# Expert weights in halves of a matrix, four neighbouring rows per partition, into pairs of slots

## The chip, the core and the metric

The kernel runs on one core of a Trainium2 chip. The core has a matrix engine (TensorE, PE in the profile), a vector engine (DVE), an activation engine (ACT, ScalarE), POOL, and a sync engine (SP) that here does nothing but issue DMAs. Sixteen DMA engines move data between HBM and the on-chip memory of 128 partitions. The metric is the time of one execution in microseconds (us).

## What is computed

Two layers, each a mixer over 256 latent and 256 context tokens of width 1024, and then 16 experts. Each expert picks 32 tokens of a stream and has three matrices of 1024 x 1024 in f32, 4 MB each. The part that the change touches:

```python
def expert_choice_ffn(h, w_router, w_g, w_u, w_d):
    ...
    aff = jax.nn.softmax(logits, axis=1)
    gate, idx = lax.top_k(aff, cap)
    xs = h[bi, idx]
    a = jnp.einsum('becd,edf->becf', xs, w_g)
    u = jnp.einsum('becd,edf->becf', xs, w_u)
    y = jnp.einsum('becf,efd->becd', jax.nn.silu(a) * u, w_d)
    return jnp.zeros_like(h).at[bi, idx].add(y * gate[..., None].astype(y.dtype))
```

In layer 0 the experts work on the latent and the context stream, in layer 1 (the last) on the latent stream alone. Before the experts comes, in each layer, `x = x + gt1 * latent_mixer(...)`: an input projection (`w_in`), attention and a short convolution, a projection per branch (`w_branch`) and an output projection (`w_out`). The modulation vectors of both come from `w_ada`.

## The kernel before

All weights pass through one arena (class `Arena`): 21 slots of 1 MB (8 KB in each partition), in the last layer's experts 22. The free slots stand in one queue and are used in the order in which they came free. `load` puts a weight's key into a list; `pump` issues the next loads of the list on SP's queue as long as a slot is free and fewer than `cap` loads are held. `cap` is set by `limit` from the table `LIMIT` (line 36) at a few points of a layer: 13, 14 and 10 around and in the experts of layer 0, 16, 17 and 17 in layer 1. A slot comes free when the last instruction that reads it has run (`done`, `give`); the DMA that takes it waits for that instruction. The list has a fixed order: the mixer's weights (`load_mixer`), then the experts' (`load_experts`), layer by layer. In the trace an expert's loads stand at L65 (one run of 8 KB per partition), all others at L68.

An expert matrix is loaded in four quarters of 256 rows (`rows`): partition p gets rows 2p and 2p + 1 of a quarter, so one packet carries 8 KB. The last expert's quarters come as two DMAs of 512 KB (4 KB rows), and the last layer's last down matrix in column halves (2 KB rows). Order of the list within expert e: gate and up quarters 1 to 3 of e, gate and up quarter 0 of e + 1, the four down quarters of e.

TensorE computes gate and up products (`gate_up`, tile gu, L1183: 8 matmuls in layer 0 for each of 8 steps k), transposes them (guT, L1280), and multiplies with the down matrix (`down` and the loop after it, tile py, L1313 in layer 0, L1232 in layer 1); xg (L1128) gathers the tokens for four experts, sc (L1216) adds the results back. Its order is written out by hand for the experts (`manual_schedule`). Since partition p holds neighbouring rows, step k has to read features in the same order: `feats(k)` picks every second column of 256. In the mixers each weight is first split into a high and a low part, `wh` on ACT (L469) and `wl` on DVE (L470), ahead of the matmuls (L439 to L441).

## Time and profile before

| | |
|---|---|
| median of 3 runs | 1789.51 us (1789.15 to 1790.28) |
| profiled execution | 1790.62 us, its span 1788.9 us |
| TensorE busy | 1628.1 us, 91% of the span |
| VectorE, ScalarE busy | 736.4 and 499.5 us |
| read from HBM | 531.21 MB, 298 GB/s over the span |
| expert loads of 1 MB | 360, 19.8 us from issue to landing (median) |

The span runs from the first to the last instruction of the profiled execution; the durations further down are from that execution, and its own time is 1.7 us longer than the span. Shares of busy time are averages over both layers' mixers and experts, so the stages are read one by one: the page cuts the span into 40 slices of 44.7 us, and a window gives the busy time, the DMA share and the rate of a stretch.

### The profile page before, as it was taken

The numbers are of one execution on the slowest core, as the hardware profiler recorded it, in microseconds if no ns is written. First come the engines' busy times: TensorE is split into PE (matmuls) and PEld (weight loads), VectorE is DVE, ScalarE is ACT, GpSimd is POOL, SyncE is SP. The second block draws the span as 40 slices with busy tenths as digits, with TensorE's granted clock in tenths as the row PEclk, the third lists the DMA queues.
The fourth block names the chain that finished last, engine by engine and source line by source line (L and its number), as shares of the span: only waits on it lengthen the run. The fifth ranks groups of instructions, "written<-read, shape, count | busy, mean of one in ns | idle before, by whom it ended". The sixth has DMA issues, their size and how long they took to land.

```text
span 1788.9 us, 23088 instructions
## 1 busy us (share of the span) xinstructions
PE 1628.1 (91%) x9134; PEld 905.5 (51%) x9134; DVE 736.4 (41%) x1678; ACT 499.5 (28%) x1081; POOL 0.6 (0%) x6
## 2 busy tenths in 40 slices
PE   7999999999999999989998899999989777778777
PEld 4886676777774343423423268878953212112111
DVE  4786775235444122221121359876662111112122
ACT  4564454223332111100101247655531000000000
POOL 0000000000000000000000000000000000000000
PEclk9999999999999999999999999999999999999999
DMA  9301124753969999999999981328788999999998
GB/s 347 111 26 48 48 71 165 236 153 118 368 226 375 391 420 421 421 421 421 421 421 419 400 321 67 118 71 238 269 337 361 421 421 421 421 421 421 422 419 338
DMA packets 131775, 533.77 MB, mean 298 GB/s; under 512 B 12452, under 2 KB 21076, under 8 KB 85588
## 3 DMA queue, kind: packets, MB, share of 16 engines
q1 hardware_dynamic: 129024, 529.90, 75.9%
q10 hardware_dynamic: 2644, 2.40, 0.4%
q8 instruction: 72, 1.18, 0.3%
q14 instruction: 35, 0.29, 0.0%
HBM read 531.21 MB, written 1.05 MB: 298 GB/s over the span
## 4 chain that ended last, share of the span: by engine, by line
PE 56%; DMA 38%; DVE 3%; ACT 2%; issue 1%; ACTq 0%; SPq 0%; DVEq 0%
DMA s<-in_w_e_up_dram 29%; DMA s<-in_w_e_down_dram 8%; PE pf L439 7%; PE pf L440 7%; PE pf L441 7%; PE gu L1183 6%; PE O L837 3%; PE S L775 2%; PE ada L306 2%; PE PTp L811 2%; PE pt L439 2%; PE pt L441 2%; PE pt L440 2%; PE sc L1216 2%; PE py L1313 2%; PE xg L1128 2%
## 5 line engine op out<-in xcount | busy, mean ns | idle before, releaser
L1183 PE MATMUL gu<-s,s 128*64 128x512 f32 (+1 forms) x1536 | 330.2, 613 | 54.7 <-DMA s<-in_w_e_up_dram 45.2
L440 PE MATMUL pf<-s,wh 128*128 128x512 f32 (+1 forms) x768 | 263.9, 344 | 0.0
L439 PE MATMUL pf<-s,wh 128*128 128x512 f32 (+1 forms) x768 | 262.9, 343 | 0.0
L441 PE MATMUL pf<-s,wl 128*128 128x512 f32 (+1 forms) x768 | 262.2, 343 | 0.0
L470 DVE TENSOR_TENSOR wl<-s,wh 128x512 fp32r<-128x512 f32 x272 | 186.0, 688 | 160.6 <-ACT wh L469 142.8
L469 ACT ACTIVATE wh<-s 128x512 fp32r<-128x512 f32 x272 | 170.4, 630 | 277.2 <-PE pf L440 193.5
L1183 PEld LDWEIGHTS gu<-s,s 128*64 128x64 f32 (+1 forms) x1536 | 90.3, 129 | 264.8 <-issue 144.5
L439 PEld LDWEIGHTS pf<-s,wh 128*128 128x128 f32 x768 | 146.1, 190 | 22.7 <-issue 5.2
L441 PEld LDWEIGHTS pf<-s,wl 128*128 128x128 f32 x768 | 145.9, 190 | 14.9 <-issue 1.8
L440 PEld LDWEIGHTS pf<-s,wh 128*128 128x128 f32 x768 | 146.3, 191 | 13.8 <-issue 0.7
L1250 ACT ACTIVATE gu<-gu 128x512 f32<-128x512 f32 x48 | 28.6, 596 | 400.6 <-PE gu L1183 400.6
L1232 PE MATMUL py<-s,aT 128*32 128x512 f32 x512 | 88.7, 624 | 39.3 <-DMA s<-in_w_e_down_dram 38.0
L1313 PE MATMUL py<-s,aT 128*32 128x512 f32 x1024 | 114.2, 594 | 2.4 <-DMA s<-in_w_e_down_dram 1.7
L1216 PE MATMUL sc<-ys,SP 128*128 128x512 f32 x192 | 93.3, 618 | 10.6 <-ACT SP L1158 7.9
L1218 DVE TENSOR_TENSOR s<-s,sc 128x512 f32<-128x512 f32 x96 | 65.9, 687 | 73.8 <-PE sc L1216 73.7
L1208 DVE TENSOR_TENSOR ys<-py,s 32x512 f32<-32x512 f32 x64 | 44.0, 687 | 126.6 <-PE py L1313 125.7
L1183 PE MATMUL gu<-s,XS 128*32 128x512 f32 x512 | 78.4, 637 | 18.1 <-DMA s<-in_w_e_up_dram 13.6
L1284 DVE TENSOR_TENSOR aT<-aT,guT 128x256 f32<-128x256 f32 x48 | 20.1, 421 | 161.7 <-ACT aT L1283 160.9
L1158 ACT ACTIVATE SP<-OGT 128x256 f32<-128x256 f32 x16 | 6.1, 383 | 265.3 <-PE OGT L1156 265.3
L1313 PEld LDWEIGHTS py<-s,aT 128*32 128x32 f32 x1024 | 31.1, 109 | 83.4 <-issue 71.1
L1204 DVE TENSOR_TENSOR ys<-py,s 128x512 f32<-128x512 f32 x32 | 20.7, 686 | 124.4 <-PE py L1232 124.4
L1232 PEld LDWEIGHTS py<-s,aT 128*32 128x32 f32 x512 | 17.5, 110 | 106.9 <-DMA s<-in_w_e_down_dram 70.5
(208 smaller groups left out, 1911.1 us busy)
## 6 DMA issues: line engine op xcount, KB each, us to landing
s<-in_w_e_gate_dram SPq DMA_DIRECT2D x120, 1024.0 KB, 19.8
s<-in_w_e_up_dram SPq DMA_DIRECT2D x120, 1024.0 KB, 19.8
s<-in_w_e_down_dram SPq DMA_DIRECT2D x120, 1024.0 KB, 19.8
s<-in_w_ada_dram SPq DMA_DIRECT2D x48, 1024.0 KB, 11.7
s<-in_w_in_dram SPq DMA_DIRECT2D x46, 1024.0 KB, 7.0
s<-in_w_branch_dram SPq DMA_DIRECT2D x16, 512.0 KB, 10.2
s<-in_w_out_dram SPq DMA_DIRECT2D x8, 1024.0 KB, 7.4
s<-in_w_e_gate_dram SPq DMA_DIRECT2D x16, 512.0 KB
```

The source lines that it names most:

```text
L439: PE.matmul(ps, lh, rh, start=start, stop=False)
L440: PE.matmul(ps, lh, rl, start=False, stop=False)
L441: PE.matmul(ps, ll, rh, start=False, stop=stop)
L469: ACT.activation(hi, w[:, kk, :], AF.Copy)
L470: DVE.tensor_tensor(out=lo, in0=w[:, kk, :], in1=hi.bitcast(F32), op=OP.subtract)
L837: PE.matmul(O[64 * kv:64 * kv + 64], v[:, k0 + kt, c0:c0 + 64], ipt[kv][1][:, kt].rearrange("p g q -> p (g q)"), start=(kt == 0), stop=(kt ...
L1183: PE.matmul(gps[fh % nf][r0:r0 + NC], XG[e // 4][1][:, k, e % 4, :], w[a][:, k % 2, 512 * fh:512 * fh + 512], start=(k == 0), stop=(k == 7))
L1208: DVE.tensor_tensor(out=ys[s][r, hs_], in0=py[r, e % 2, :], in1=g2[s][r, hs_], op=OP.mult)
L1216: PE.matmul(po, w, ys[s][:, hs_], start=True, stop=True)
L1218: DVE.tensor_tensor(out=o, in0=o, in1=po, op=OP.add)
L1232: PE.matmul(py[r0:r0 + 32, h, :], aT[:, ff, :], rhs, start=(ff < 4), stop=(ff >= 4))
L1313: PE.matmul(py[r0:r0 + 32, e % 2, :], aT[:, ff, 32 * s:32 * s + 32], w[:, ff % 2, 512 * h:512 * h + 512], start=(ff == 0), stop=(ff == 7))
```

## The change

A matrix is loaded in two halves of 512 rows; partition p gets rows 4p to 4p + 3 of a half, so a packet carries 16 KB and a load 2 MB. The 21 slots become ten pairs, p0 to p9, and one single slot; a load of an expert half takes a whole free pair (`take_two`), 1 MB loads take the free half of a pair that is already open if there is one (`take`). `cap` counts slots; in layer 1 it is 18 in place of 17. `feats`, the router's weights, the ffn's bias and gain vectors (`wst`, `wt`) follow the new order of features; two more small transposes at the start prepare them. In layer 1 the hand-written order of the steps is kept by calling `gate_up` for two steps at a time. The last expert's halves come in four DMAs of 512 KB, 4 KB rows as before, and all gate parts of a half come ahead of its up parts. The last down matrix keeps its 2 KB rows. Cut to its core:

```diff
-LIMIT = [(8, 2, 13, 14, 10), (8, 6, 16, 17, 17)]
+LIMIT = [(8, 2, 13, 14, 10), (8, 6, 16, 18, 18)]
...
+    def open(self, j, dtype):
+        self.tiles[j] = (self.pool.tile([128, 4096], dtype, name=f"p{j}", tag=f"pair{j}"), dtype)
+
+    def fits(self, i, dtype):
+        j = i // 2
+        return i >= self.n // 2 * 2 or j not in self.tiles or self.tiles[j][1] == dtype
+
+    def take(self, shape, dtype, name, alone=False):
+
+
+        ok = [i for i in self.free if self.fits(i, dtype)]
+        pairs = [i for i in ok if i < self.n // 2 * 2]
+        single = [i for i in ok if i not in pairs]
+        i = next((k for k in pairs if k // 2 in self.tiles), (pairs or single)[0])
+        if alone and single:
+            i = single[0]
+        self.free.remove(i)
+        return i, self.view(i, shape, dtype)
...
+    def drop(self, us):
+        self.free.extend(us)
+        for i in us:
+            if i ^ 1 in self.free and i // 2 in self.tiles:
+                del self.tiles[i // 2]
+
+    def take_two(self):
+
+        seen = set()
+        for i in self.free:
+            if i ^ 1 in seen and i < self.n // 2 * 2:
+                a = i & ~1
+                self.free.remove(a)
+                self.free.remove(a + 1)
+                return a
+            seen.add(i)
+        return None
...
+    def load_rows(self, key, w, parts):
+
+        self.queue.append((key, w.rearrange("(p k) f -> p k f", k=4), parts, 2))
...
+            w, parts = shape, src
+            a = self.take_two()
+            if a is not None:
+                us = [a, a + 1]
+            else:
+                us = ([i for i in self.free if self.fits(i, F32)] if force else self.odd())[:2]
+                if len(us) < 2:
+                    return False
...
+                whole = self.tiles[a // 2][0]
+            ts = [self.view(u, [128, 2, D], F32) for u in us]
+            if parts > 1:
+                for k in range(4):
+                    self.nc.sync.dma_start(out=ts[k // 2][:, k % 2], in_=w[:, k])
+            elif a is not None:
+                self.nc.sync.dma_start(out=whole, in_=w.rearrange("p k f -> p (k f)"))
+            else:
...
-        while self.queue and self.free and len(self.ready) < self.cap:
-            self._issue()
+        while self.queue and len(self.free) >= self.queue[0][3] and self.held + self.queue[0][3] <= self.cap:
+            if not self._issue():
+                return
...
-    def rows(key, w, q, parts):
-
-        w = w[256 * q:256 * q + 256]
-        if parts == 1:
-            ar.load(key, [128, 2, D], w.rearrange("(p k) f -> p (k f)", k=2), "p k f -> p (k f)")
-        else:
-            w = w.rearrange("(p k) f -> p k f", k=2)
-            ar.load(key, [128, 2, D], [((slice(0, 128), i), w[:, i]) for i in range(2)])
 
...
-                rows((nm, l, e, q), w[l, e], q, 2 if e == NE - 1 else 1)
+                ar.load_rows((nm, l, e, q), w[l, e, 512 * q:512 * q + 512], 2 if e == NE - 1 else 1)
 
         up(0, 0)
         for e in range(NE):
 
             parts = 2 if e == NE - 1 else 1
-            for q in range(1, 4):
-                up(e, q)
+            up(e, 1)
             if e + 1 < NE:
                 up(e + 1, 0)
-            if (l, e) != (DEPTH - 1, NE - 1):
-                for q in range(4):
-                    rows(("d", l, e, q), w_e_down[l, e], q, parts)
-                continue
-            for h in range(2):
-                w = w_e_down[l, e, :, 512 * h:512 * h + 512].rearrange("(q p k) f -> q p k f", p=128, k=2)
-                for i in range(2):
-                    ar.load(("d", l, e, h, i), [128, 4, 512],
-                            [((slice(0, 128), slice(2 * q, 2 * q + 2)), w[2 * i + q]) for q in range(2)])
+            for i in range(2):
+                w = w_e_down[l, e, 512 * i:512 * i + 512]
+                if (l, e) != (DEPTH - 1, NE - 1):
+                    ar.load_rows(("d", l, e, i), w, parts)
+            if (l, e) == (DEPTH - 1, NE - 1):
+                for h in range(2):
+                    w = w_e_down[l, e, :, 512 * h:512 * h + 512].rearrange("(q p k) f -> q p k f", p=128, k=4)
+                    for i in range(2):
+                        ar.load(("d", l, e, h, i), [128, 4, 512], w[i])
...
-        return slice(256 * (k // 2) + k % 2, 256 * (k // 2) + 256, 2)
+        return slice(512 * (k // 4) + k % 4, 512 * (k // 4) + 512, 4)
...
-        for i in range(4):
-            q.dma_start(out=wr[:, 2 * i:2 * i + 2, 0:NE],
-                        in_=w_router[l, 256 * i:256 * i + 256].rearrange("(p k) e -> p k e", k=2))
+        for i in range(2):
+            q.dma_start(out=wr[:, 4 * i:4 * i + 4, 0:NE],
+                        in_=w_router[l, 512 * i:512 * i + 512].rearrange("(p k) e -> p k e", k=4))
...
-        def gate_up(e, q, ks=(0, 1)):
+        def gate_up(e, q, ks=(0, 1, 2, 3)):
             if q == 0 and 0 in ks:
                 for f0 in range(nf):
                     gps[f0] = pmm([128, 512], "gu")
             keys = [(nm, l, e, q) for nm in ("g", "u")]
             w = [ar.get(key) for key in keys]
-            for k in (2 * q + i for i in ks):
+            for i in ks:
+                k = 4 * q + i
                 for fh in range(2):
                     for a in range(2):
                         r0 = NC * (a + 2 * (fh // nf))
                         PE.matmul(gps[fh % nf][r0:r0 + NC], XG[e // 4][1][:, k, e % 4, :],
-                                  w[a][:, k % 2, 512 * fh:512 * fh + 512], start=(k == 0), stop=(k == 7))
-            if 1 in ks:
+                                  w[a][i][:, 512 * fh:512 * fh + 512], start=(k == 0), stop=(k == 7))
+            if 3 in ks:
                 for key in keys:
                     ar.done(key)
 
         one_hot(0)
         gather(0, 0)
         gate_up(0, 0)
-        gate_up(0, 1)
...
-            for q in range(2 if e == 0 else 1, 4):
-                gate_up(e, q)
-
-                if last and e and q == (1 if e == NE - 1 else 2):
+            if e:
+                gate_up(e, 0, (2, 3))
+
+                if last:
+                    if e < NE - 1:
+                        gate_up(e, 1, (0, 1))
                     way_back(e - 1)
                     scatter(e - 1, 0)
                     scatter(e - 1, 1)
+            gate_up(e, 1, (2, 3) if last and 0 < e < NE - 1 else (0, 1, 2, 3))
...
-                for q in (0, 2):
+                for q in range(2):
                     for h in range(2):
-                        down(e, py, h, (q, q + 1))
-                    for i in (q, q + 1):
-                        ar.done(("d", l, e, i))
+                        down(e, py, h, (q,))
+                    ar.done(("d", l, e, q))
             else:
-                for q in range(4):
+                for q in range(2):
                     w = ar.get(("d", l, e, q))
-                    for ff in range(2 * q, 2 * q + 2):
+                    for ff in range(4 * q, 4 * q + 4):
                         for h in range(2):
                             for s in range(ns):
                                 r0 = 32 * block(e, s, h)
                                 PE.matmul(py[r0:r0 + 32, e % 2, :], aT[:, ff, 32 * s:32 * s + 32],
-                                          w[:, ff % 2, 512 * h:512 * h + 512], start=(ff == 0), stop=(ff == 7))
+                                          w[ff % 4][:, 512 * h:512 * h + 512], start=(ff == 0), stop=(ff == 7))
                     ar.done(("d", l, e, q))
             for h in range(2):
```

On TensorE, ACT and DVE the order of the instructions stays as it was but for the two transposes and a few neighbours that change places. What moves is SP's row of loads. Names are tiles: s8 is slot 8, p1 pair 1, the number behind it a running number, which says how late in the program the load stands.

SP, the first expert loads of layer 0, before: each goes into a slot that a mixer weight left.

```order
L68 DMA s4_4287<-in_w_ada_dram 128x4x512
L65 DMA s8_4289<-in_w_e_gate_dram 128x2048
L65 DMA s9_4308<-in_w_e_up_dram 128x2048
L65 DMA s10_4374<-in_w_e_gate_dram 128x2048
L65 DMA s3_4503<-in_w_e_up_dram 128x2048
L65 DMA s19_4505<-in_w_e_gate_dram 128x2048
L65 DMA s20_4549<-in_w_e_up_dram 128x2048
L65 DMA s6_4551<-in_w_e_gate_dram 128x2048
L65 DMA s1_4568<-in_w_e_up_dram 128x2048
```

SP, the same place after: each takes a pair, eight different ones, and then p1 and p0 a second time.

```order
L129 DMA p7_2701<-in_w_ada_dram 128x4x512
L151 DMA p1_4282<-in_w_e_gate_dram 128x4096
L151 DMA p0_4415<-in_w_e_up_dram 128x4096
L151 DMA p6_4459<-in_w_e_gate_dram 128x4096
L151 DMA p3_4476<-in_w_e_up_dram 128x4096
L151 DMA p5_4489<-in_w_e_gate_dram 128x4096
L151 DMA p8_4511<-in_w_e_up_dram 128x4096
L151 DMA p9_4596<-in_w_e_down_dram 128x4096
L151 DMA p7_4598<-in_w_e_down_dram 128x4096
L151 DMA p1_4638<-in_w_e_gate_dram 128x4096
L151 DMA p0_4659<-in_w_e_up_dram 128x4096
```

The first load has moved to about where the second stood, but is twice as large, and the second half matrix (p0_4415) stands behind the third quarter.

SP, the end of layer 1's mixer, before: all mixer loads (the last are `w_ada`) stand ahead of the experts'.

```order
L68 DMA s14_9727<-in_w_out_dram 128x4x512
L68 DMA s10_9867<-in_w_ada_dram 128x4x512
L68 DMA s19_9945<-in_w_ada_dram 128x4x512
L68 DMA s3_9947<-in_w_ada_dram 128x4x512
L65 DMA s6_9949<-in_w_e_gate_dram 128x2048
L65 DMA s2_9951<-in_w_e_up_dram 128x2048
L65 DMA s12_9953<-in_w_e_gate_dram 128x2048
```

SP, the same place after:

```order
L151 DMA p5_9612<-in_w_e_up_dram 128x4096
L129 DMA p9_6807<-in_w_out_dram 128x4x512
L129 DMA p3_9160<-in_w_out_dram 128x4x512
L129 DMA p2_4539<-in_w_ada_dram 128x4x512
L129 DMA p7_6500<-in_w_ada_dram 128x4x512
L129 DMA p2_4539<-in_w_ada_dram 128x4x512
L151 DMA p0_9614<-in_w_e_gate_dram 128x4096
L129 DMA p4_3977<-in_w_ada_dram 128x4x512
L151 DMA p9_9750<-in_w_e_up_dram 128x4096
L151 DMA p1_9788<-in_w_e_gate_dram 128x4096
```

The first expert loads stand between the mixer's last; two pairs (p9, p3) still take mixer weights there.

SP, the output projection's weights (`w_out`) at the end of layer 0's mixer, before: each in a slot of its own.

```order
L68 DMA s14_3957<-in_w_out_dram 128x4x512
L68 DMA s15_3943<-in_w_ada_dram 128x4x512
L68 DMA s8_4043<-in_w_ada_dram 128x4x512
L68 DMA s4_4034<-in_w_out_dram 128x4x512
L68 DMA s9_4045<-in_w_ada_dram 128x4x512
L68 DMA s17_4090<-in_w_ada_dram 128x4x512
L68 DMA s10_4047<-in_w_out_dram 128x4x512
L68 DMA s11_4049<-in_w_out_dram 128x4x512
```

SP, the same place after:

```order
L129 DMA p2_131<-in_w_branch_dram 64x4x512 x2
L129 DMA p4_3977<-in_x_dram 128x2x1024
L129 DMA p7_2701<-in_w_ada_dram 128x4x512
L129 DMA p8_3484<-in_w_ada_dram 128x4x512
L129 DMA p2_131<-in_w_out_dram 128x4x512
L129 DMA p4_3977<-in_ctx_dram 128x2x1024
L129 DMA p7_2701<-in_w_out_dram 128x4x512
```

The first two output weights now go into halves of the open pairs p2 and p7 and stand behind other loads into the same pairs; the other two stand much further ahead, in p0.

## Rows read from the trace of the kernel before

**Rows 1.** The page's 40 slices: busy tenths, and the rate.

```profile
PE   7999999999999999989998899999989777778777
DMA  9301124753969999999999981328788999999998
GB/s 347 111 26 48 48 71 165 236 153 118 368 226 375 391 420 421 421 421 421 421 421 419 400 321 67 118 71 238 269 337 361 421 421 421 421 421 421 422 419 338
```

**Rows 2.** The page's chain that ended last, by engine and by line.

```profile
PE 56%; DMA 38%; DVE 3%; ACT 2%; issue 1%; ACTq 0%; SPq 0%; DVEq 0%
DMA s<-in_w_e_up_dram 29%; DMA s<-in_w_e_down_dram 8%; PE pf L439 7%; PE pf L440 7%; PE pf L441 7%; PE gu L1183 6%; PE O L837 3%; PE S L775 2%; PE ada L306 2%; PE PTp L811 2%; PE pt L439 2%; PE pt L441 2%; PE pt L440 2%; PE sc L1216 2%; PE py L1313 2%; PE xg L1128 2%
```

**Rows 3.** TensorE's waits, 560:1050 and 1340:1790: total us, times, longest.

```profile
PE gu L1183 <- DMA s<-in_w_e_up_dram: 21.4, 19, 1.5
...
PE py L1232 <- DMA s<-in_w_e_down_dram: 38.0, 34, 2.8
```

**Rows 4.** Windows: us, PE PEld DVE ACT POOL busy, PE clock, DMA share, GB/s.

```profile
485.00:500.00 15.00, 15.00 (x68) 12.48 (x69) 5.66 (x10) 3.34 (x7) 0.00 (x0) 1.00 1.05 386
990.00:1005.00 15.00, 11.15 (x50) 3.35 (x47) 2.75 (x4) 0.00 (x0) 0.00 (x0) 1.00 1.03 409
650.00:900.00 250.00, 237.49 (x1390) 89.78 (x1386) 50.45 (x91) 26.93 (x56) 0.00 (x0) 1.00 1.01 421
1400.00:1700.00 300.00, 225.35 (x1164) 59.81 (x1164) 54.45 (x100) 17.29 (x38) 0.00 (x0) 0.96 1.01 421
```

**Rows 5.** SP's timeline, start of layer 0's experts: start, us, line, DMA, count.

```profile
551.36 0.33 SPq L65 DMA_DIRECT2D s<-in_w_e_gate_dram  x1
567.00 0.33 SPq L65 DMA_DIRECT2D s<-in_w_e_up_dram  x1
...
570.44 0.33 SPq L65 DMA_DIRECT2D s<-in_w_e_up_dram  x1
...
590.52 0.33 SPq L65 DMA_DIRECT2D s<-in_w_e_gate_dram  x1
```

**Rows 6.** Windows of the same stretch, columns as in rows 4.

```profile
509.00:590.00 81.00, 77.58 (x451) 45.06 (x447) 30.18 (x94) 23.78 (x48) 0.00 (x0) 1.00 0.81 317
590.00:626.00 36.00, 36.00 (x226) 12.18 (x216) 7.50 (x12) 2.94 (x6) 0.00 (x0) 1.00 1.01 421
```

**Rows 7.** TensorE's timeline, layer 0's first experts: start, us, line, tile, count.

```profile
563.33 7.09 PE L1183 MATMUL gu<-s,s 128*64 128x512 f32 x32
...
604.27 1.09 PE L1166 MATMUL OGT<-ident,OG 128*128 128x128 f32 x8
605.30 1.94 PE L1183 MATMUL gu<-s,s 128*64 128x512 f32 x8
607.16 1.23 PE L1280 MATMUL guT<-ident,gu 128*128 128x128 f32 x8
```

**Rows 8.** TensorE by line, 769.7:890.3, four experts: busy, mean ns, idle before.

```profile
L1183 PE MATMUL gu<-s,s 128*64 128x512 f32 x259 | 62.9, 599 | 9.4 <-DMA s<-in_w_e_up_dram 8.3 <-DMA s<-in_w_e_gate_dram 1.0
```

**Rows 9.** SP's timeline, start of layer 1's experts.

```profile
1333.97 0.33 SPq L65 DMA_DIRECT2D s<-in_w_e_up_dram  x1
1346.96 0.33 SPq L65 DMA_DIRECT2D s<-in_w_e_gate_dram  x1
```

**Rows 10.** A window of the same stretch, columns as in rows 4.

```profile
1344.00:1348.00 4.00, 4.00 (x38) 1.81 (x40) 0.82 (x2) 0.92 (x2) 0.00 (x0) 1.00 0.13 20
```

**Rows 11.** TensorE's timeline there.

```profile
1345.00 3.64 PE L1183 MATMUL gu<-s,XS 128*32 128x512 f32 x32
```

**Rows 12.** TensorE's timeline at the end of layer 0's experts.

```profile
1002.43 3.65 PE L1183 MATMUL gu<-s,s 128*64 128x512 f32 x14 [1.47 <-DMA s<-in_w_e_up_dram]
```

**Rows 13.** SP's timeline in layer 0's mixer.

```profile
352.00 1.27 SPq L68 DMA_DIRECT2D s<-in_w_branch_dram  x2
...
445.57 0.37 SPq L68 DMA_DIRECT2D s<-in_w_out_dram  x1
```

**Rows 14.** Layer 0's mixer: a wait of ACT (270:500), DVE's timeline at 382.

```profile
ACT wh L469 <- DMA s<-in_w_branch_dram: 2.6, 1, 2.6
...
382.02 0.69 DVE L470 TENSOR_TENSOR wl<-s,wh 128x512 fp32r<-128x512 f32 x1 [2.03 <-ACT wh L469]
```

More of the change, by code (lines that the diff above doesn't have):

```diff
@@ L46, in __init__, with view @@
         self.ready = {}
-        self.cap = 0
-        self.extra = {}
-    def take(self, shape, dtype, name):
-        i = self.free.popleft()
-        return i, self.extra.get(i, self.pool).tile(shape, dtype, name=f"s{i}", tag=f"slot{i}")
+        self.cap = self.held = 0
+    def view(self, i, shape, dtype):
+        n = 1
+        for k in shape[1:]:
+            n *= k
+        if i >= self.n // 2 * 2:
+            t = (self.last if i == self.n else self.pool).tile([128, 2048], dtype, name=f"s{i}", tag=f"slot{i}")
+        else:
+            if i // 2 not in self.tiles:
+                self.open(i // 2, dtype)
+            t = self.tiles[i // 2][0][:, 2048 * (i % 2):2048 * (i % 2) + 2048]
+        t = t[:, 0:n]
+        if len(shape) == 3:
+            return t.rearrange("p (a b) -> p a b", a=shape[1])
+        if len(shape) == 4:
+            return t.rearrange("p (a b c) -> p a b c", a=shape[1], b=shape[2])
+        return t
@@ L81, in get, with pop @@
         while key not in self.ready:
-            self._issue()
+            if not self._issue(True):
+                raise RuntimeError(f"no room for {key}")
         return self.ready[key][1]
+    def pop(self, key):
+        us, t = self.ready.pop(key)
+        self.held -= len(us)
+        return us[0], t
     def done(self, key):
-        self.give(self.ready.pop(key)[0])
+        us = self.ready.pop(key)[0]
+        self.held -= len(us)
+        self.drop(us)
+        self.pump()
 @with_exitstack
```

77 lines of the change are left out of this document (47 added, 30 removed).

## The prediction

> **What bounds the kernel now.** I read the page's slices first, then the chain of work that ended last, then windows. In the slices the kernel has two halves of a layer: in the mixers (0 to about 505 us, 1050 to 1330) TensorE is full and the DMA engines are not, in the experts (about 590 to 1010 and 1350 to 1780) the DMA row stands at 9 and the rate at 421 GB/s [rows 1]. The chain says the same: 38% of the span is DMA, nearly all of it expert weights [rows 2]. Where TensorE waits in the experts it waits for a weight matrix that has not landed: 21.4 us for up matrices in layer 0, 38.0 us for down matrices in layer 1 [rows 3]. So the end of a layer's experts is set by two things: when the stream of weights starts to flow without a gap, and how long one MiB takes. TensorE's granted clock there is 0.96 to 1.00 [rows 4], the level of 2.4 GHz, so it is not the question. The rate depends on the row that a packet carries: windows with a DMA share of 1.01 or more give 386 GB/s where mixer weights with rows of 2 KB land, 409 for the last expert's 4 KB rows, 421 for the 8 KB rows of the others, in both layers [rows 4].
>
> **Gain: the longer row.** Sixteen engines at those rates take 84.9, 160.2 and 311.3 ns for a packet of 2, 4 and 8 KB (bytes x 16 over the rate). That is a straight line: 75.3 and 75.55 ns per 2 KB between neighbours, and 9.6 or 9.1 ns that do not grow. Carried on, a 16 KB packet takes 612.5 to 613.5 ns where two of 8 KB take 622.6: 9.1 to 10.1 ns less, about 428 GB/s. No row of before has such packets under load, so the far bounds are 0 ns (a packet of 16 KB as dear as two) and, from the line without its constant part (4 x 151.1 = 604.4 ns), 18 ns. I take 9.6, the middle of the line's two readings. Fifteen experts of a layer use it, 12 MiB each, 180 MiB per layer; the last expert keeps its short rows. What counts is only what flows after the stream has become gapless: 158 MiB in layer 0 and 162 in layer 1 (below), that is 10,112 and 10,368 packets, 632 and 648 per engine. 1280 x 9.6 ns = **12.3 us** of gain (11.6 to 12.9; far bounds 0 and 23).
>
> The Trainium skill (DMA: Bandwidth & Descriptors, "Where 436 GB/s comes from") puts the ceiling into SBUF at 435 GB/s. The line's slope, 75.5 ns per 2 KB, is 434, so the trace agrees; at the ceiling itself a 16 KB packet would take an estimated 602.6 ns and the gain would be 25.6 us.
>
> **Cost: the start of the stream in layer 0.** A load may start when its room is free. Before, every 1 MB slot that a mixer weight leaves is filled at once; now a load needs both halves of a pair, and half a matrix is 2 MB. For each early load of the changed order I looked up which instruction frees its second half and when that instruction ended in the trace of before. Before, 14 loads of 1 MB are out by 547.6 and 17 by 551.4; the next wait for TensorE's first expert products, until 567.0 [rows 5]. From 509 to 590 the core moved 317 GB/s, 24.5 MiB, of which about 0.8 MiB by my count of the packets were mixer weights still landing: 23.7 MiB of experts; after 590 it runs at 421 [rows 6], so 24.3 at 591.5. After, the 2 MB loads get their room at 522.5, 523.9, 533.4, 540.5, 544.5, 547.6, 549.3 and 551.3 (eight), then at 570.4 (two, when the first 32 products end [rows 7]), 581.6 and 590.5, instants at which before issues loads too [rows 5]. The queue empties before 570.4, before 581.6 and before 590.5, since 2 MB need 5 us. With 1 us from issue to data, 22 MiB are down when the twelfth begins at 591.5, and from there the queue always holds a load. 2.3 MiB behind, at 0.4015 MiB per us: **5.7 us**. TensorE is not stalled by that at once: its products for experts 0 to 3 find their data until about 673, as I follow them down [rows 7]; from there it waits as before, since an expert takes it 27.8 us (the 120.6 us of four experts less 9.4 of waiting for DMA, over four [rows 8]) and the DMA 29.4.
>
> **Cost: the start in layer 1.** Here too the stream stops: 20 loads are out by 1334.0, the next wait until 1347.0 [rows 9], and the core moves 20 GB/s from 1344 to 1348 [rows 10]. After, nine pairs (the new cap of 18) are out by 1333.1, and the next needs the products of expert 0 that end at 1348.6 [rows 11]: data at 1349.7 against 1347.9 before. By 1349.7 before has 20.4 MiB (20.0 and the first 1.8 us, ramp taken off), after 18: 2.4 MiB, **5.9 us**. Room after that is freed by TensorE every few us as far ahead as before.
>
> **Cost: the tails.** Last expert of layer 0: gate parts all come ahead of up parts now, and its third and fourth products have to be done after expert 14's down product. Before, two products of 3.65 us end 3.65 us after the last up part [rows 12]; after, six products (three times 3.65 us) follow that down product, and I get an end 0.2 to 0.6 us later. I take **0.4 us**. Layer 1's last down matrix has 2 KB rows in both; cost 0.
>
> **Edits without a price.** The same matmuls, activations and vector operations run in the same order; two more transposes of a 12-row tile at the start lie under the first loads. Reading features four apart and not two apart: eight transposes take 1.23 us at a stride of two against 1.09 us for a tile read in a row [rows 7], so 0.14 us at most per expert for the next doubling, under the 1.6 us per expert that TensorE still waits. On SP's queue 368 instructions replace 554 at 0.33 us each, which no one waits for.
>
> Mixer 0's weights move too, since the free list now fills half-open pairs first and keeps whole pairs for the experts. Some eight loads are issued 13 to 45 us later: the branch weight of 352.0 goes to 380.0, the first output weight of 445.6 to 467.0 [rows 13]. Splitting on ScalarE and VectorE runs 9 to 11 us ahead of TensorE in this stretch, and such a load costs it up to 5, so I count 0. Without that cover each late weight costs 1 to 5 us; before shows one such wait of ScalarE, 2.6 us [rows 14].
>
> **Sum.** -12.3 + 5.7 + 5.9 + 0.4 = -0.3 us against the profiled execution's 1790.6 (span 1788.9 and 1.7 around it), which lies 1.1 above the median: **1789.2 us** on the median's scale. A measurement of this kernel can tell about 0.2%, 3.6 us, from no change.
>
> **Rivals.**
> 1. *The row gains more than the line says.* The line is fitted on three points and the gain is far from its bound of 18 ns per packet: 1280 x 18 = 23 us less 12.0 gives 1778.5; halfway, 1784. For: each doubling so far gained. Against: the constant part was 9.1 to 9.6 ns at both steps.
> 2. *The stream is not late.* Both start costs rest on instants of before; if the mixers' last weights leave their pairs earlier, or if the loads that I let wait share the queue better, half of 11.6 us goes: 1783.4. For: the freed instants are those of TensorE, and the free list can pick other pairs. Against: the gaps of layer 1 stand in before too, at one slot's grain [rows 10].
>    The Trainium skill (Perfetto Trace Analysis, "DMA Optimizations") has a rule for each side: larger DMAs saturate the memory better, and splitting lets some start sooner where the engines idle. This kernel's windows show both, full engines after 590 and idle ones before; by the first alone the time would be 1777, by the second alone 1801.5.
> 3. *A packet of 16 KB gains nothing* (it is cut up on the way, or two of 8 KB already hide their constant part). Then only the costs stay: +12.0, **1801.5**, slower. It decides from the rate of the gapless stretch: below 421.5 GB/s it is this one. Against: 386 to 409 to 421.
> 4. *Mixer 0's late weights stall TensorE.* ScalarE's split of a late branch or output weight holds up what is queued behind it in ScalarE, softmax included. Two or three of the eight at 2 us: +5, 1794.5. It decides where an issue moves to within 5 us of the split (380.0 against the first split of that branch weight at 382.0 [rows 14]).
>
> **How the numbers follow.** Forecast (no change, own range 1786 to 1792): 0.46. Rival 1: 0.14, rival 2: 0.18, rival 3: 0.09, rival 4: 0.13. Faster by over 0.2%: 0.14 + 0.18 = 0.32; slower: 0.09 + 0.13 = 0.22; within: 0.46. For 8 in 10 the range takes in rival 2, the near half of rival 1 and rival 4, and leaves out the far ends of 1 and 3: 1780 to 1798.
>
> **What would show it.** Gapless windows in layers 0 and 1 at 427 to 429 GB/s. In layer 0 the DMA share of 509 to 590 falls and three short gaps stand between 560 and 592; in layer 1 the gap at 1344 is about 2 us longer. TensorE's first long wait for a weight comes near 673 again. The mixer of layer 0 ends within 1 us of before. Last loads of either layer land within 1.5 us of before. It is wrong if the rate is under 424 or over 432, or if TensorE first enters the experts late.

## The result: 1815.4 us, 1.4% slower

| | before | after |
|---|---|---|
| median | 1789.33 us (1789.01 to 1790.28, 4 runs) | 1815.44 us (1811.73 to 1816.85, 4 runs) |
| ratio, 95% interval | | 1.0142 (1.0129 to 1.0154) |
| profiled execution, its span | 1790.62, 1788.9 us | 1811.73, 1809.9 us |
| TensorE busy | 1628.1 us | 1646.0 us |

The forecast was 1789.2 us, no change, with a range of 1780 to 1798. The change costs 26.1 us.

The slices of after, which answer to [rows 1]:

```profile
PE   7999999999999999999999899999988867777767
...
DMA  9211124744867899999999992236778999999998
GB/s 332 98 49 47 47 70 155 229 140 143 307 253 317 347 410 427 428 422 427 422 428 422 407 334 94 95 93 175 262 310 358 428 428 427 427 428 427 427 423 333
```

Where the stream of weights is gapless it is faster, 427 or 428 GB/s for 421. But in the middle of layer 0's experts two slices stand at 422 between others at 427 and 428, so there the stream waits; and TensorE's row, which had three 8s from there to the end of these experts, has one. The chain that ended last, which answers to [rows 2], says the same:

```profile
PE 70%; DMA 24%; DVE 3%; ACT 2%; issue 1%; ACTq 0%; SPq 0%; DVEq 0%
PE gu L1272 13%; DMA p<-in_w_e_down_dram 11%; DMA p<-in_w_e_up_dram 9%; PE pf L527 7%; PE pf L528 7%; PE pf L529 7%; PE py L1403 5%; PE xg L1216 4%; DMA p<-in_w_e_gate_dram 3%; PE O L925 3%; PE sc L1304 3%; PE S L863 2%; PE PTp L899 2%; PE ada L395 2%; PE pt L527 2%; PE pt L529 2%
```

DMA has fallen from 38 to 24% of the span, and TensorE has risen from 56 to 70, with the gather of the tokens (xg) at 4% for 2. TensorE's waits in 560:1050 (total us, times, longest) answer to [rows 3]:

```profile
PE py L1403 <- DMA p<-in_w_e_down_dram: 8.4, 5, 3.4
PE gu L1272 <- DMA p<-in_w_e_up_dram: 5.4, 3, 2.1
```

13.8 us of waiting for weights where before had 21.4 for the up matrices alone. In layer 0 it is TensorE that has become slower. The groups by line (busy us, mean ns of one, idle before) name the place. Before:

```profile
L1128 PE MATMUL xg<-OH,s 128*128 128x128 f32 x384 | 50.7, 290 | 1.8 <-ACT OH L1119 1.7
...
L1128 PEld LDWEIGHTS xg<-OH,s 128*128 128x128 f32 x384 | 48.2, 202 | 9.5 <-issue 4.2 <-ACT OH L1119 2.6 <-ACT gu L1250 2.4
...
L1280 PEld LDWEIGHTS guT<-ident,gu 128*128 128x128 f32 x192 | 25.5, 208 | 27.2 <-issue 14.0 <-ACT gu L1250 8.3 <-ACT s L1137 4.1
...
L349 PE MATMUL abp<-sel,rows 128*128 128x2 f32 x96 | 12.1, 247 | 0.0
```

After:

```profile
L1216 PE MATMUL xg<-OH,p 128*128 128x128 f32 x384 | 93.3, 402 | 1.8 <-ACT OH L1207 1.8
L1216 PEld LDWEIGHTS xg<-OH,p 128*128 128x128 f32 x384 | 90.8, 329 | 9.3 <-issue 4.2 <-ACT OH L1207 2.7 <-ACT gu L1341 2.4
...
L1371 PEld LDWEIGHTS guT<-ident,gu 128*128 128x128 f32 x192 | 25.7, 210 | 26.6 <-issue 12.3 <-ACT gu L1341 9.4 <-ACT p L1225 2.4
...
L438 PE MATMUL abp<-sel,rows 128*128 128x2 f32 x96 | 19.1, 321 | 0.2 <-ACT rows L397 0.2
```

The matmuls that gather the tokens take 402 ns and not 290, and those that turn a modulation row into columns (abp) 321 and not 247. In both, the operand that is read by `feats`, now every fourth feature and not every second, is the stationary one, which LDWEIGHTS loads, and its load went from 202 to 329 ns. The transposes guT read the same stride and stayed at 208 to 210. Busy time: +42.6 us for the gathers, +7.0 for abp.

Where this meets the path is in TensorE's timeline (start, us, line, tile, count; answers to [rows 7]). Before:

```profile
558.46 4.94 PE L1128 MATMUL xg<-OH,s 128*128 128x128 f32 x36 [0.38 <-ACT OH L1119]
```

After:

```profile
565.27 8.67 PE L1216 MATMUL xg<-OH,p 128*128 128x128 f32 x36 [0.38 <-ACT OH L1207]
573.87 7.09 PE L1272 MATMUL gu<-p,p 128*64 128x512 f32 x32
580.89 6.80 PE L1216 MATMUL xg<-OH,p 128*128 128x128 f32 x28
```

The first gather starts at 565.27 (before 558.46) and takes 8.67 us (before 4.94 for the same 36 matmuls). The products whose end frees the next pairs end at 581.0, not 570.4, 10.5 us late; the second gather, 6.80 us for 28 matmuls, follows. Windows (us, PE PEld DVE ACT POOL busy, PE clock, DMA share, GB/s), which answer to [rows 6] and [rows 4]:

```profile
509.00:592.00 83.00, 79.10 (x408) 52.09 (x408) 32.65 (x99) 20.16 (x45) 0.00 (x0) 1.00 0.70 278
592.00:626.00 34.00, 33.43 (x204) 11.85 (x204) 5.50 (x10) 8.52 (x15) 0.00 (x0) 1.00 0.78 318
650.00:900.00 250.00, 243.67 (x1334) 106.61 (x1334) 53.25 (x100) 28.02 (x59) 0.00 (x0) 1.00 1.00 423
...
1440.00:1700.00 260.00, 189.87 (x1038) 62.97 (x1038) 49.40 (x91) 15.93 (x35) 0.00 (x0) 0.91 1.01 427
```

From 592 to 626, where before ran at 421, it is 318. By my count of the packets 19.6 MiB of expert weights are down at 592 (before 24.5) and 29.9 at 626 (before 38.1), and the last 4 KB row lands at 1029.5 in layer 0 (before 1013.4) and 1790.4 in layer 1 (before 1770.0). So 16 us of the loss arise in layer 0, and layer 1 adds about 4. (The profiled execution of after is the fastest of its four, 21.1 us above before's.)

### The profile page after: what moved, and what is told of

The parts are those of the page before. It is cut to its first block, busy times and chain, and to the rows that moved or that the text cites. A ratio compares the mean times of both kernels' runs of the same rounds, so it can differ in the third digit from the quotient of the medians.

```text
span 1809.9 us, 22641 instructions
## 1 busy us (share of the span) xinstructions
PE 1646.0 (91%) x9136; PEld 955.0 (53%) x9136; DVE 736.5 (41%) x1678; ACT 496.3 (27%) x1081; POOL 0.6 (0%) x6
## 3 DMA queue, kind: packets, MB, share of 16 engines
HBM read 531.21 MB, written 1.05 MB: 294 GB/s over the span
## 4 chain that ended last, share of the span: by engine, by line
PE 70%; DMA 24%; DVE 3%; ACT 2%; issue 1%; ACTq 0%; SPq 0%; DVEq 0%
PE gu L1272 13%; DMA p<-in_w_e_down_dram 11%; DMA p<-in_w_e_up_dram 9%; PE pf L527 7%; PE pf L528 7%; PE pf L529 7%; PE py L1403 5%; PE xg L1216 4%; DMA p<-in_w_e_gate_dram 3%; PE O L925 3%; PE sc L1304 3%; PE S L863 2%; PE PTp L899 2%; PE ada L395 2%; PE pt L527 2%; PE pt L529 2%
## 5 line engine op out<-in xcount | busy, mean ns | idle before, releaser
L527 PE MATMUL pf<-p,wh 128*128 128x512 f32 (+1 forms) x768 | 262.4, 343 | 0.0
L528 PE MATMUL pf<-p,wh 128*128 128x512 f32 (+1 forms) x768 | 262.4, 342 | 0.0
L529 PE MATMUL pf<-p,wl 128*128 128x512 f32 (+1 forms) x768 | 261.8, 342 | 0.0
L558 DVE TENSOR_TENSOR wl<-p,wh 128x512 fp32r<-128x512 f32 x272 | 184.8, 688 | 148.4 <-ACT wh L557 141.2
L1272 PE MATMUL gu<-p,p 128*64 128x512 f32 x1024 | 234.8, 597 | 5.9 <-DMA p<-in_w_e_up_dram 5.4
L557 ACT ACTIVATE wh<-p 128x512 fp32r<-128x512 f32 x272 | 169.1, 629 | 249.3 <-PE pf L528 147.0
L527 PEld LDWEIGHTS pf<-p,wh 128*128 128x128 f32 x768 | 145.3, 189 | 22.2 <-issue 5.5
L528 PEld LDWEIGHTS pf<-p,wh 128*128 128x128 f32 x768 | 145.6, 190 | 14.5 <-issue 1.3
L529 PEld LDWEIGHTS pf<-p,wl 128*128 128x128 f32 x768 | 145.2, 189 | 14.6 <-issue 1.5
L1403 PE MATMUL py<-p,aT 128*32 128x512 f32 x1024 | 114.0, 594 | 9.2 <-DMA p<-in_w_e_down_dram 8.4
L1320 PE MATMUL py<-p,aT 128*32 128x512 f32 x512 | 72.9, 700 | 48.9 <-DMA p<-in_w_e_down_dram 47.6
L1216 PEld LDWEIGHTS xg<-OH,p 128*128 128x128 f32 x384 | 90.8, 329 | 9.3 <-issue 4.2
L1216 PE MATMUL xg<-OH,p 128*128 128x128 f32 x384 | 93.3, 402 | 1.8 <-ACT OH L1207 1.8
```

The source lines that it names most:

```text
L527: PE.matmul(ps, lh, rh, start=start, stop=False)
L528: PE.matmul(ps, lh, rl, start=False, stop=False)
L529: PE.matmul(ps, ll, rh, start=False, stop=stop)
L557: ACT.activation(hi, w[:, kk, :], AF.Copy)
L558: DVE.tensor_tensor(out=lo, in0=w[:, kk, :], in1=hi.bitcast(F32), op=OP.subtract)
L1216: PE.matmul(pt[:, j, :], (Y if g else X)(2 * s + t)[:, feats(4 * h + j)], OH[:, 2 * s + t].rearrange("p e c -> p (e c)"), start=(t == 0), ...
```

## The experiments

The first theory, A in the expectations: reading the stationary operand four features apart is what costs, and the rest of the change comes out near the forecast. Its rival: the late start of the stream (2 MB loads into pairs) costs more than was forecast, and the slower gathers are covered.

### Undo the stride, keep the rest

The changed kernel with neighbouring features in the two reads. This gathers features in another order than the weights have.

```diff
+    def flat(k):
+        return slice(128 * k, 128 * k + 128)
...
-            PE.matmul(ps[:, b, :], rows[:, feats(b)] if kind > 2 else rows[:, 128 * b:128 * b + 128], sel2[:, 0:2],
+            PE.matmul(ps[:, b, :], rows[:, flat(b)] if kind > 2 else rows[:, 128 * b:128 * b + 128], sel2[:, 0:2],
...
-                        PE.matmul(pt[:, j, :], (Y if g else X)(2 * s + t)[:, feats(4 * h + j)],
+                        PE.matmul(pt[:, j, :], (Y if g else X)(2 * s + t)[:, flat(4 * h + j)],
```

> The changed kernel with one thing undone: the token gather (xg) and the modulation columns (abp) read 128 features side by side as their stationary operand, not every fourth one. The features then come in the wrong order, so the output is not the reference's; loads, order and amount of work are those of the changed kernel. Theory A (the weight load that reads every fourth f32, 16 bytes apart, is the loss: xg 402 ns a matmul against 290 before, 42.6 us more in all, abp 7 us more): xg falls to 290 ns or below, abp to 247, TensorE is at its first gather within 2 us of before (558.5 us, against 565.3 in the changed kernel), and the time is 1788 to 1794 us, what the first prediction gave without this term. Theory B (loads of 2 MB start late and starve TensorE): xg gets shorter, but the stream's gaps stay and the time stays above 1805 us.

Measured: 1796.07 us (1794.88 to 1798.84), 1.0038 of before (1.0024 to 1.0053).

```profile
L1220 PE MATMUL xg<-OH,p 128*128 128x128 f32 x384 | 48.3, 284 | 2.0 <-ACT OH L1211 1.8 <-DVE p L1227 0.2
...
L1220 PEld LDWEIGHTS xg<-OH,p 128*128 128x128 f32 x384 | 45.8, 197 | 9.7 <-issue 4.2 <-ACT OH L1211 2.7 <-ACT gu L1345 2.4
```

```profile
592.00:626.00 34.00, 34.00 (x212) 11.59 (x206) 7.50 (x12) 2.94 (x6) 0.00 (x0) 1.00 0.99 413
650.00:900.00 250.00, 233.15 (x1326) 87.48 (x1324) 51.05 (x92) 26.92 (x56) 0.00 (x0) 1.00 1.01 427
```

The gather is at 284 ns, the stretch 592:626 at 413 GB/s, and 22.0 MiB are down at 592. 19.4 of the 26.1 us are gone. abp is back at 244 ns, and the first gather starts at 559.96, 1.5 us after before's. The time misses theory A's 1788 to 1794 by 2 us: what is left, 6 to 7 us net of the longer row's gain, is not the stride's and not in the forecast either.

### The stride alone, in the kernel before

```diff
+    def four_apart(k):
+        return slice(512 * (k // 4) + k % 4, 512 * (k // 4) + 512, 4)
...
-                        PE.matmul(pt[:, j, :], (Y if g else X)(2 * s + t)[:, feats(4 * h + j)],
+                        PE.matmul(pt[:, j, :], (Y if g else X)(2 * s + t)[:, four_apart(4 * h + j)],
```

and the same for abp; loads, slots and order are those of before.

> The kernel before with that one thing added: xg and abp read every fourth feature, not every second; loads as before, 1 MB with 8 KB rows. The features come in the wrong order, so the output is not the reference's. Theory A: xg rises from 290 to about 400 ns and abp from 247 to 320; TensorE's four experts in layer 0 then need 111.2 + 7.4 = 118.6 us against 119.6 us of DMA, and the first gathers of both layers delay the stream: 1799 to 1812 us. Theory B: 1789 to 1793 us, since the loads are those of before.

Measured: 1806.00 us (1805.44 to 1812.16), 1.0100 of before (1.0083 to 1.0117): +16.0 us. The gather's matmuls in the groups by line, and two windows:

```profile
L1132 PE MATMUL xg<-OH,s 128*128 128x128 f32 x384 | 93.0, 402 | 1.3 <-ACT OH L1123 1.3
L1132 PEld LDWEIGHTS xg<-OH,s 128*128 128x128 f32 x384 | 90.9, 328 | 9.1 <-issue 4.2 <-ACT gu L1254 2.4 <-ACT OH L1123 2.4
```

```profile
566.00:580.00 14.00, 14.00 (x63) 10.40 (x64) 2.33 (x5) 2.56 (x7) 0.00 (x0) 0.89 0.27 107
650.00:900.00 250.00, 245.08 (x1372) 106.83 (x1376) 53.52 (x100) 28.46 (x60) 0.00 (x0) 1.00 1.00 414
```

402 ns again, with a hole in the stream at 566 to 580 (107 GB/s) that before doesn't have, and in 650:900 a stream of 414 GB/s that waits for TensorE at times, although not one load has changed. This profiled execution is the slowest of the four, 6.2 us above the median, and its granted clock falls to 1.2 GHz here:

```profile
556.00:568.00 12.00, 10.84 (x26) 5.82 (x25) 5.35 (x16) 1.31 (x5) 0.00 (x0) 0.50 1.01 418
```

TensorE had been busy without a pause from 540 to 555. So the size of that hole is this execution's; after has its hole (570 to 580 at 88 GB/s) at a clock of 1.00. The time is inside theory A's range and the gathers are where it put them: theory A holds. The stride costs 16.0 us in the kernel before and 19.4 in the changed one.

### The longer row alone

The kernel of the first experiment, but a pair is loaded by two DMAs of 1 MB with 8 KB rows:

```diff
-            elif a is not None:
-                self.nc.sync.dma_start(out=whole, in_=w.rearrange("p k f -> p (k f)"))
```

> As the run with side-by-side features, and each half matrix is loaded in two DMAs of 1 MB with 8 KB rows into the same pair of slots: the grain of 2 MB without the longer packet. The output is not the reference's for the same reason. If a 16 KB packet saves 9.6 ns against two of 8 KB, as the line through 2, 4 and 8 KB says, the gapless windows fall from 427.5 to 421 GB/s and the time is 10 to 14 us above that run (1280 packets per engine, 12.3 us). If the rate is not what limits, within 3 us of it.

Measured: 1806.14 us (1801.45 to 1809.42), 1.0091 of before (1.0072 to 1.0110), 10.1 us above the same kernel with 16 KB rows.

```profile
650.00:900.00 250.00, 233.36 (x1310) 88.08 (x1306) 49.64 (x89) 26.16 (x54) 0.00 (x0) 0.99 1.01 421
```

421 GB/s where the first experiment has 427. So the longer row does gain: 10.1 us where 12.3 were forecast. The intervals of the two runs leave some 4 us either way, so 12.3 is not excluded.

### The slot rule alone

The kernel before with all its loads (1 MB, 8 KB rows, two features apart, cap 17); only the 21 slots are handed out as in the changed kernel: ten pairs and a single one, halves of open pairs first.

```diff
-        i = self.free.popleft()
-        return i, self.extra.get(i, self.pool).tile(shape, dtype, name=f"s{i}", tag=f"slot{i}")
+        ok = [i for i in self.free if self.fits(i, dtype)]
+        pairs = [i for i in ok if i < self.n // 2 * 2]
+        single = [i for i in ok if i not in pairs]
+        i = next((k for k in pairs if k // 2 in self.tiles), (pairs or single)[0])
...
```

> The kernel before with all its loads as they were (1 MB, 8 KB rows, features two apart, cap 17 in layer 1), but its 21 slots handed out by the changed kernel's rule: ten pairs and a single slot, a load takes the free half of an open pair first. Theory F (the rule alone delays loads, which is what cost the kernel with only the down matrices in halves its 9 us): 1794 to 1799 us, a gap of 4 us or more in the stream between 560 and 571 and one in layer 1 that is longer than the 4.9 us of before; the gathers stay at 290 ns a matmul, the rate at 421. Theory G (the rule is harmless as long as loads are of 1 MB; what costs is the need for two free halves at once): 1789 to 1791.5 us, the gap in layer 1 as before, and no new gap ahead of 590.

Measured: 1798.15 us (1797.07 to 1799.88), 1.0047 of before (1.0033 to 1.0060): +8.0 us with every load as it was. The rule has two parts, the order in which slots are handed out and the joining of two slots in one tile; this run does not separate them. Before at 560:571, then this kernel:

```profile
560.00:571.00 11.00, 10.86 (x63) 5.77 (x62) 1.64 (x4) 1.83 (x4) 0.00 (x0) 1.00 0.83 331
```

```profile
560.00:571.00 11.00, 10.51 (x64) 6.51 (x66) 2.33 (x5) 3.00 (x8) 0.00 (x0) 1.00 0.34 125
```

The stream has a hole there, 125 GB/s for 331. SP's timeline at the start of layer 1's experts, which answers to [rows 9]:

```profile
1336.29 0.33 SPq L129 DMA_DIRECT2D p<-in_w_e_gate_dram  x1
1349.55 0.80 SPq L129 DMA_DIRECT2D p<-in_w_e_up_dram  x2
```

18 loads of expert weights are out by 1336.3, then none until 1349.55; before has 20 out by 1334.0 and goes on at 1346.96. Two MiB less and 2.6 us later come to 7.6 us by 0.4015 MiB per us. The last 4 KB row of the kernel lands 7.5 us later than before's (1777.5 for 1770.0, counted from the packets), and that of layer 0 2.6 us later (1016.0 for 1013.4). Theory F holds.

### The halves for the down matrices alone

The kernel before with the pairs and the slot rule; gate and up matrices in quarters, two features apart, down matrices in halves of 16 KB rows, and the cap of layer 1 is 18. Gathers and abp stay as before; only guT reads four apart.

```diff
-                for q in range(4):
-                    rows(("d", l, e, q), w_e_down[l, e], q, parts)
...
+            for i in range(2):
+                w = w_e_down[l, e, 512 * i:512 * i + 512]
+                if (l, e) != (DEPTH - 1, NE - 1):
+                    ar.load_rows(("d", l, e, i), w, parts)
...
-                    PE.transpose(pt[:, j, :], gu[:, feats(j)], ident)
+                    PE.transpose(pt[:, j, :], gu[:, slice(j, 512, 4)], ident)
```

> The kernel before with the change made for the down matrices alone: they come in halves of 2 MB with 16 KB rows into pairs of slots, gate and up stay in quarters of 1 MB with 8 KB rows, so the gathers and the modulation columns read every second feature as before. Only the transposes of the hidden features read four apart, and those took 1.23 us for eight at either stride. 60 MiB per layer save 9.6 ns per 16 KB packet: 480 packets per engine, 4.6 us. Theory A: 1785 to 1788 us. If a strided read four apart cost the same in the transposes, or pairs are hard to get beside single slots: 1790 to 1796.

Measured: 1798.54 us (1796.63 to 1801.29), 1.0048 of before (1.0036 to 1.0061). The expectation was wrong, and its second range too: I had counted the row's gain and no cost of the rule, and the rule alone (the run above) stands at 1798.15. That the 4.6 us of gain do not show either suggests that loads which need two free halves cost about as much again; no run shows that cost alone. At the boundary of the layers TensorE's timeline shows two late `w_ada` loads. Before at the same place, then this kernel:

```profile
1030.76 0.69 PE L410 MATMUL yT<-ident,s 128*128 128x128 f32 x2 [4.91 <-DVE s L404]
```

```profile
1030.94 1.06 PE L401 MATMUL ada<-p,sact 128*32 128x512 f32 x8 [1.75 <-DMA p<-in_w_ada_dram]
1034.38 1.89 PE L401 MATMUL ada<-p,sact 128*32 128x512 f32 x2 [2.37 <-DMA p<-in_w_ada_dram]
```

They cost little: before waits 4.91 us for VectorE there. From the end of the scatter (sc) to the first yT it takes 6.8 us, this kernel 8.0 and the rule alone, with the same two waits, 7.6.

### Smaller pieces for the first experts

The kernel of the first experiment with the first two experts of each layer in pieces of 1 MB:

```diff
+    def load_two(key, w, h):
+        ar.load(key + (h,), [128, 2, D], w.rearrange("(p k) f -> p k f", k=4)[:, 2 * h:2 * h + 2])
...
+            if e < EARLY:
+                for h in range(2):
+                    for nm, w in (("g", w_e_gate), ("u", w_e_up)):
+                        load_two((nm, l, e, q), w[l, e, 512 * q:512 * q + 512], h)
+                return
```

> The run with side-by-side features (1796 us; output not the reference's for that order of features), and the first two experts of each layer are loaded in pieces of 1 MB with 8 KB rows into single slots, everything after them in 2 MB with 16 KB rows. Theory C (what is left of the loss after the strided reads is the coarse start of the stream, 2.3 MiB in layer 0 and 2.3 in layer 1, 5.6 to 5.9 us each): the expert bytes landed at 592 us return from 22.0 to about 24 MiB, the gap at 1349 shrinks, and the time falls by 6 to 10 us, to 1786 to 1790. Rival D (the rest comes from the mixers' late weights and from the boundary between the layers): less than 3 us, 1793 to 1796.

Measured: 1792.20 us (1788.37 to 1794.99, 10 runs), 1.0011 of before (1.0002 to 1.0020). 23.0 MiB are down at 592 for 22.0. That is 3.9 us less than the first experiment, between the two expectations, so it settles neither; a late start is part of the rest.

### Mending it: sorted copies of the tokens

Both reads can be in a row if the tokens lie in the weights' order. ScalarE writes such copies ahead of the first gather, where the kernel before wrote plain copies of them behind it:

```diff
+                ACT.activation(Y(t)[:, 512 * h:512 * h + 512].rearrange("p (k a) -> p a k", k=4),
+                               X(t)[:, 512 * h:512 * h + 512].rearrange("p (a k) -> p a k", k=4), AF.Copy,
+                               scale=nst[:, 3, t:t + 1])
...
-                        PE.matmul(pt[:, j, :], (Y if g else X)(2 * s + t)[:, feats(4 * h + j)],
+                        PE.matmul(pt[:, j, :], Y(2 * s + t)[:, flat(4 * h + j)],
```

> The changed kernel with a right order of features and no strided weight load: ScalarE writes the scaled copy of the tokens, which the later gathers read anyway, ahead of the first gather and with the features already sorted, and sorts the modulation rows where it copies them from PSUM. All gathers then read 128 neighbours. Theory A: xg at 290 ns, the time within 4 us of the run with side-by-side features if ScalarE's eight copies (about 5 us) lie under the top-k of VectorE, up to 6 us more if they don't. Theory B: above 1805 us.

Measured: 1804.51 us (1802.42 to 1806.63), 1.0084 of before (1.0069 to 1.0099). The gathers are at 281 ns, so theory A has the matmul right, but the time is 8.4 us above the first experiment. ScalarE's and TensorE's timelines:

```profile
544.37 6.08 ACT L1169 ACTIVATE p<-p,nst 128x512 f32<-128x512 f32 x6
550.24 1.11 ACT L400 ACTIVATE rows<-ada 128x512 f32<-128x512 f32 x2
```

```profile
552.34 1.05 PE L445 MATMUL abp<-sel,rows 128*128 128x2 f32 x8 [1.05 <-ACT rows L398]
...
562.34 4.87 PE L1225 MATMUL xg<-OH,p 128*128 128x128 f32 x32
```

Six copies stand ahead of the modulation rows that TensorE's abp waits for, and the first gather starts at 562.34, 2.4 us after that of the first experiment (559.96). That is not the whole of the 8.4 us, and the copies are not the only thing that differs. This execution too is the slowest of its four, and after the wait of 1.05 us its clock falls to 1.2 GHz, where the first experiment has 1.00:

```profile
555.00:564.00 9.00, 8.62 (x24) 5.12 (x23) 4.32 (x15) 0.54 (x1) 0.00 (x0) 0.50 1.01 431
```

The copies' tiles also take slots of the arena ahead of the first products and not behind them, and 19.4 MiB of expert weights are down at 592 for the first experiment's 22.0. What each of the three costs was not separated.

The same copies on POOL, which does nothing else there, together with the early experts in 1 MB:

> A kernel with the right order of features: as the run with sorted copies (1804.5 us), but POOL, which is idle, writes the sorted copies of the tokens and not ScalarE, and the first two experts come in 1 MB pieces. In that run ScalarE's eight copies of 1.05 us delayed the modulation rows behind them, and the first gather began at 562.3 us against 558.5 before. If POOL's copies end before the first one-hot matrix is ready, the first gather is back at 560 and the time at 1788 to 1793; if POOL takes over 1.5 us for each of the eight copies, or slows VectorE's top-k beside it, 1795 to 1803.

Measured: 1789.98 us (1786.97 to 1795.94, 10 runs), 0.9998 of before (0.9988 to 1.0007). POOL's timeline:

```profile
546.03 16.78 POOL L1181 TENSOR_SCALAR p<-p,nst 128x512 f32<-128x512 f32 x8 [544.86 <-DMA s<-in_b_ada_dram]
```

Eight copies in 16.8 us, ending 1 us ahead of the first gather at 563.77. The time is the one expected, but not for the reason given: in the profiled execution POOL takes 2.1 us for each copy, over the 1.5 that were to make it 1795 or more, and the first gather is not back at 560. That execution is the slowest of the ten, 6 us above the median, and its mixer ends 5.4 us later than the first experiment's (the transposes behind it, xT, start at 509.67 for 504.29), so it doesn't show where the median's time comes from. Against the changed kernel the sorted copies on POOL and the early 1 MB pieces together give 25.5 us back, about all that the change had cost.

Last, the same kernel with the early 1 MB loads in the slot that has been free longest:

```diff
-        i = next((k for k in pairs if k // 2 in self.tiles), (pairs or single)[0])
+        i = next((k for k in pairs if k // 2 in self.tiles), (pairs or single)[0]) if near else ok[0]
```

> The correct kernel with sorted copies of the tokens written by POOL and the first two experts in 1 MB pieces, but these pieces take the slot that has been free longest, not the second half of a pair that is already open. If the order in which slots are handed out holds up the early loads: the gap ahead of 590 shrinks by 2 us or more and the time falls to 1785 to 1788 us. If the mixer's last instructions free the room at the same instants whichever slot is taken: 1788.5 to 1791.5 us, no different from the kernel with the pairs filled first (1789.98).

Measured: 1788.49 us (1787.11 to 1792.68, 11 runs), 0.9996 of before (0.9987 to 1.0005). The hole ahead of 592 is shorter (579.3 to 582.2 where the kernel above has 568.3 to 572.9), by 1.7 us and not the 2 expected, and the time can't be told from that of the kernel above. The mixer's weights, and the 2 MB loads behind, still go by the rule; whether that is the reason was not tested. No version was found that beats the kernel before by more than can be measured.

## Why the prediction was wrong, step by step

The parts in a ladder, each a median against the one above it: before 1790.18 in those runs; the slot rule +8.0 (1798.15); the rest of the change at 8 KB rows, +8.0 (1806.14), probably above all loads that need two free halves at once, though the cap of 18 and the order of the last expert's loads are in it too; 16 KB rows -10.1 (1796.07); features four apart +19.4 (1815.44). The rungs were measured at different times and are uncertain by some 2 to 4 us either way. The kernels at 1806.14 and 1796.07 also have neighbouring features, whose gathers take 46.8 and 48.3 us of busy time for 50.7 two apart.

- **The step that failed** is the one among the edits without a price: "Reading features four apart and not two apart ... 0.14 us at most per expert for the next doubling, under the 1.6 us per expert that TensorE still waits". Both halves were wrong. The bound came from a transpose, and transposes do not slow at four apart; the gathers, which hold the same stride in an ordinary matmul, do. 64 of them per four experts, 112 ns each, are 7.2 us, 1.8 per expert. That is more than the cover of 1.6: four experts take TensorE 111.2 + 7.2 = 118.4 us, and 48 MiB at 427 GB/s take 117.9. But that excess is small. Most of the loss is where there is no cover at all, ahead of the experts, where abp and the first gathers stand before the products that free the next pairs: against the first experiment abp brings the first gather 5.3 us later, the first 36 gathers take 3.8 us more and the next 28 take 3.4 more. At 626 the stream is 5.2 MiB, 12.8 us, behind the first experiment's, of the 13.9 us by which layer 0's last 4 KB row lands later (1029.5 for 1015.6). The nearest row was that of the gathers themselves; what they take at four apart no row of before shows, and the text should have kept that open above.
- **The row.** 427 to 428 GB/s as forecast (427 to 429). A packet of 16 KB takes 16384 x 16 / 427.5 = 613 ns, as forecast; the gain was 10.1 us for 12.3, within what the runs can tell. Rivals 1 and 3 fall.
- **The start in layer 0.** 22 MiB at 591.5 were forecast, 22.0 at 592 came, but only with the stride undone. In after the products that free the pairs are 10.5 us late, and it is 19.6.
- **The starts together** were priced at 11.6 us. Without the row and the stride the change costs 16.1 (1806.14 against 1790.02), so with the tails' 0.4 these terms were too small by some 4. The packets of the first experiment say where: layer 0's stream is 3.0 MiB behind before's at 626 (7.5 us for 5.7), and layer 1's, as forecast 2.4 behind at 1349.7, is 4.2 behind at 1372 (10.4 us, 2.2 of them from layer 0's later end, so 8.2 for 5.9). What failed in layer 1 is "Room after that is freed by TensorE every few us as far ahead as before". Rival 2, that the stream is not late, falls. The slot rule alone costs 8.0, and the prediction treated it under mixer 0 alone; it holds back loads in layer 1 also with 1 MB loads.
- **Mixer 0's late weights**, counted as 0 with rival 4 beside it: a late load does stall the mixer, but it is a `w_ada` load that TensorE waits for, 1.4 us once in layer 0, in after and with the stride undone. The first gather of the first experiment starts 1.5 us later than before's. So the rival's size was about 1.5 and not 5, and by another weight than it named.
- **The tails**, 0.4 us: no run separates them.
- Of what was to show it, the rate held, the mixer's end did not (the first gather came 6.8 us late, most of it by abp, since the first experiment has 1.5 and the 80 abp matmuls ahead of that gather took 15.2 us for 10.0), nor did the last loads (16.1 and 20.4 us later). TensorE's first wait for an expert weight, forecast near 673, came at 664 in the first experiment and at 742 in after (before has it at 727). It named what would make it wrong, "if TensorE first enters the experts late", and that is what happened.

The Trainium skill (Advanced Engine Details and Errata, "SBUF Cachelines") says that SBUF has lines of 16 bytes and that a line needs at least two hits for full speed. f32 values two apart put two into a line, four apart one: the weight loads of the gathers, 202 and 329 ns, agree. The transposes' loads, 208 and 210 ns, do not show it. That rule spoke against this change, and the prediction left it out.

## What to carry to other kernels

A layout that makes a transfer longer often makes an on-chip read wider-strided: look for every matmul that reads through it, by operand, and price it from a row of that same kind of instruction, not from one that looks alike. Work ahead of the instruction that frees a buffer has no cover, even where the engine has slack later. And the order in which free buffers are handed out is an edit with a price of its own: measure it alone before the larger transfers that it is made for.

## What the runs showed of the hardware

- An f32 weight load of 128 columns takes 197 ns from neighbouring elements (192 to 198 over the runs that read so), 202 from every second (201 to 205) and 329 from every fourth; the matmul that it belongs to 284, 290 and 402. A transpose's weight load of the same size takes 208 at two apart and 210 at four. Why transposes are spared is open; no run tells.
- Packets of 2, 4, 8 and 16 KB flow at 386, 409, 421 and 427 to 428 GB/s: the part of a packet's time that does not grow with its length, 9.6 ns by the shorter rows, is 9.4 by the step from 8 to 16 KB.
- In layer 1 (1440:1700) the granted clock, a mean of pieces at 2.4 GHz and at 1.2 GHz, is 0.91 in after and 0.88 in the first and third experiments, whatever their row, where before shows 0.96 and the slot rule alone 0.97. TensorE's waits there come in fewer and longer pieces with 2 MB loads. For the up matrices (us in total, times, longest), before and the first experiment:

```profile
PE gu L1183 <- DMA s<-in_w_e_up_dram: 37.4, 34, 1.5
```

```profile
PE gu L1276 <- DMA p<-in_w_e_up_dram: 49.3, 14, 3.9
```

What that clock costs was not measured; the stream sets the pace there.
